# Plain float32 TensorE steps of a GLA stage put next to each other, and the end of the cross samples' chain moved into that stage

## The chip, the cores and the metric

The kernel runs on one core of one Trainium2 chip. The metric is the device time of one execution in microseconds (us). Three executions of the kernel before took 1443.68 us in the median (1443.25 to 1445.27). A fourth was taken with the hardware profiler: 1445.01 us, with a span of 1443.3 us from the first to the last instruction on the core.

## What is computed

One layer of a hybrid decoder, for 1024 prompt tokens and 8 sample tokens (one token each, with caches), width 1024. All branches read the same normalised input:

```python
h = rmsnorm(x, norm_gain)
q, k, v, gla_g, a_lr, u, pool_g, xq, xg, merge = split(h @ w_in)
z = a_lr @ w_a2 + b_a                       # the "logits" of the forget gate, rank 16
log_a = log_sigmoid(z) / 16
o, S = gla_chunked(q, k, v, log_a, S0)      # gated linear attention, 4 heads, 128 x 256
p, new_hist = multiscale_pool(u, hist, ...) # trailing means, a linear map for each of 4 groups
c = cross_attn(xq, mem_k, mem_v)            # 4 heads of 256, 256 memory tokens
merged = sum over the branches of sigmoid(merge) * (branch * silu(gate)) @ w_branch
y = rmsnorm(x + merged @ w_out, final_gain)
```

Outputs are both `y`, the prompt's memory keys and values, and the new GLA and pool states.

## The kernel before, in words

**The spine.** The input projection is 40 column blocks ("pairs") of `w_in`, each done as seven products of blocks (a scheme of Strassen's kind). `seq` lists 280 products, `run_product` (L547) does one. A product has two halves; a half (`product`, L537) is 12 matmuls of 128x258, four times the three of `mm3` (L240: hi*hi, hi*lo, lo*hi, lines 242 to 244). The operands of `mm3` are float32r: a value is split into a rounded half and a rest (`split`, L220: one ScalarE copy, one VectorE subtraction, lines 223 and 224), and three float32r products stand for one float32 product.

**What is woven in.** After each half product, `fill` (L1244) runs a little of a side stream. A stream is a Python generator that emits some instructions and yields a cost; `Stream.run` (L1229) takes steps until the sum of the costs reaches 493 * (half - 28) / 329, so about 1.5 of cost go with one half. All steps that fall to one half are emitted with no half between them. Stream 0 is `mix`: first `cross_steps` (cross-attention of the prompt, with the samples' chain `cross_sample` woven in), then `gla_steps` (GLA of the prompt, with `gla_sample` woven in). Stream 1, `pool_steps`, begins when stream 0 is over.

**What sets the order.** The order on TensorE and on the SyncE queue (SP: all loads) is the order in which the program emits. The orders of VectorE (DVE), ScalarE (ACT) and GpSimd (POOL) are picked at build time by a list scheduler. Every engine runs its list in order.

**The GLA stage before.** There are 16 chunks n of 256 tokens (4 heads x 4). For each n, `gla_steps` (L1069) does, with a yield behind each:
- `gla_gates(n+1)` (L904; 5): one plain float32 matmul of 128x256 (L907, the logits), then a long chain of 12 VectorE and 7 ScalarE steps that ends in L935, the scaled keys;
- `gla_split(n)` and `gla_within` of the first half of chunk n (L938; 2): two float32 matmuls on column tiles of 64 (L944, L945), a float32 transpose of the scaled keys (L946), a mask (L947), a split into `ak`;
- `gla_recur` of the second half of chunk n-1 (L952; 2): six float32r matmuls, and one plain float32 one (L963) with the state;
- `gla_within` of the second half of chunk n (2); the loads of n+2 and n+1 and `gla_recur` of the first half of chunk n (2); `gla_out(n-1)` (2).
Steps of the sample chain stand between them, one or two at a place.

**The cross stage's end.** Steps s = 0 to 17 emit scores(s), values(s-2) and weights(s-1), and five steps of `cross_sample` for each s. For s = 16 and 17 there are no scores left, and what is left of the last head's chain (softmax of the samples L791 to L798, its transpose L803, two groups of matmuls on column tiles of 32, L817, a last transpose L827) follows closely.

**Banks.** The side streams share two PSUM banks (`PZ`, tag pz) in turn; a bank comes free when ACT or DVE has read what the second last tile held. The spine has six (`PX`).

Of the kernel before, what the change touches and what calls it, by code (L numbers as in the profile page):

```python
# [18 lines left out]
P = 128  # L19
# [5 lines left out]
NH = 4  # L25
# [8 lines left out]
CT = 256  # L34
# [13 lines left out]
def trunk_kernel(ctx: ExitStack, tc: tile.TileContext,  # L48
# [3 lines left out]
    nc = tc.nc  # L52
# [46 lines left out]
    def PZ():  # L99
        return ps.tile([P, 512], F32, tag="pz", name="pz", bufs=2)  # L100
# [87 lines left out]
    w2 = cp.tile([P, 512], F32, name="w2")  # L188
# [488 lines left out]
    def perm8(ap):  # L677
        return ap.rearrange("p (i j) -> p i j", i=2)

    cross = {}  # L680

    def cross_load(h):
        cross["raw", h] = [loaded(mkv_scr[o][h], [2, DV], "mkv") for o in range(2)]
# [16 lines left out]
    def cross_scores(h, c):  # L700
        xh, xl = cross["q", h, c]
        mh, ml = cross["mk", h]
        t = PZ()
        for j in range(2):
            for i in range(2):
                cs = slice(j * P, (j + 1) * P)
                mm3(t[:, j * NM:(j + 1) * NM], xh[:, i, cs], xl[:, i, cs], mh[:, i], ml[:, i], i == 0, i == 1)
        nm = tiny(2, "nm")
        nc.vector.tensor_reduce(nm, t.rearrange("p (j m) -> p j m", j=2), axis=AX.X, op=ALU.max, negate=True)
        p = R([2, NM], name="p")  # L710
        sm = tiny(2, "sm")
        for j in range(2):
            act(p[:, j], t[:, j * NM:(j + 1) * NM], AF.Exp, bias=nm[:, j:j + 1], accum_out=sm[:, j:j + 1])
        nc.vector.reciprocal(sm, sm)
        for j in range(2):
            nc.vector.tensor_scalar(p[:, j], p[:, j], sm[:, j:j + 1], None, op0=ALU.mult)
        cross["p", h, c] = p
# [114 lines left out]
    def cross_steps():  # L832
        def scores(n):
            cross_scores(n // 4, n % 4)

        def memory(n):
            if n % 4 == 0:
                cross_memory(n // 4)

        def weights(n):  # L840
            cross_weights(n // 4, n % 4)

        def values(n):
            cross_values(n // 4, n % 4)

        samples = chain_of(cross_sample(h) for h in range(NH))
        cross_load(0)
        cross_memory(0)
        cross_fetch(0, 0)
        yield 2  # L850
        cross_queries(0, 0)
        cross_fetch(0, 1)
        for s in range(16 + 2):
            if s < 16:
                scores(s)
                yield 3
                if s + 1 < 16:
                    cross_queries(*divmod(s + 1, 4))
                if s + 2 < 16:
                    cross_fetch(*divmod(s + 2, 4))  # L860
            if s % 4 == 2 and s < 14:
                cross_load(s // 4 + 1)
            if s >= 1:
                yield next(samples, 0)
            if 0 <= s - 2:
                values(s - 2)
                yield 1.7
            if s >= 1:
                yield next(samples, 0)
            if s % 4 == 3 and s < 15:  # L870
                memory(s + 1)
                yield 2
            if 0 <= s - 1 < 16:
                weights(s - 1)
                yield 1.7
            for _ in range(3):
                if s >= 1:
                    yield next(samples, 0)
        yield from samples

    def chain_of(gens):
        for g in gens:
            yield from g


    gla = {}
# [9 lines left out]
    def gla_load(h, c):  # L896
        alc = wk.tile([P, CT], F32, tag="alc", name="alc", bufs=2)
        nc.sync.dma_start(out=alc, in_=al_scr[c // 2][:, (c % 2) * CT:(c % 2 + 1) * CT])
        kq = R([2, CT], name="kq")
        for j, scr in enumerate((k_scr, q_scr)):  # L900
            nc.sync.dma_start(out=kq[:, j], in_=scr[h // 2][:, 2 * (h % 2) + c // 2, (c % 2) * CT:(c % 2 + 1) * CT])
        gla["in", h, c] = alc, kq

    def gla_gates(h, c):  # L904
        alc, kq = gla["in", h, c]
        t = PZ()
        nc.tensor.matmul(t[:, :CT], lhsT=w2[:, h * P:(h + 1) * P], rhs=alc, start=True, stop=True)  # L907
        bz = R([2, CT], name="bz")
        b, z = bz[:, 0], bz[:, 1]
        gate_exps(t[:, :CT], CT, h, z, b)  # L910
        nc.vector.tensor_tensor_scan(b, smask, b, 0.0, op0=ALU.mult, op1=ALU.add)
        bl = b.rearrange("p (c e t) -> p c e t", e=2, t=64)[:, :, :, 63]
        dec = wk.tile([P, 4], F32, tag="dec", name="dec", bufs=3)
        d2 = dec.rearrange("p (c e) -> p c e", e=2)
        act(d2, bl, AF.Exp, scale=1.0 / TAU)
        decp = wk.tile([P, 2], F32, tag="decp", name="decp", bufs=3)
        nc.vector.tensor_tensor(decp, d2[:, :, 0], d2[:, :, 1], op=ALU.mult)
        blp = wk.tile([P, 4], F32, tag="blp", name="blp", bufs=2)
        blp2 = blp.rearrange("p (c e) -> p c e", e=2)
        nc.vector.tensor_copy(blp2[:, :, 1], bl[:, :, 1])  # L920
        nc.vector.tensor_tensor(blp2[:, :, 0], bl[:, :, 0], bl[:, :, 1], op=ALU.add)
        k, q = kq[:, 0], kq[:, 1]
        kiqi = R([2, CT], name="kiqi")
        ki, qi = kiqi[:, 0], kiqi[:, 1]
        act(z, b, AF.Exp, scale=1.0 / TAU, bias=lnq_c)
        nc.vector.tensor_tensor(q, q, z, op=ALU.mult)
        q4, qi4 = (x.rearrange("p (a e t) -> p a e t", e=2, t=64) for x in (q, qi))
        nc.vector.tensor_copy(qi4[:, :, 0], q4[:, :, 0])
        nc.vector.tensor_tensor(qi4[:, :, 1], q4[:, :, 1], d2[:, :, 0:1].to_broadcast([P, 2, 64]), op=ALU.mult)
        act(z, b, AF.Exp, scale=-1.0 / TAU)  # L930
        nc.vector.tensor_tensor(ki, k, z, op=ALU.mult)
        nc.vector.tensor_tensor(z.rearrange("p (c t) -> p c t", t=64), blp[:, :, None].to_broadcast([P, 4, 64]),
                                b.rearrange("p (c t) -> p c t", t=64), op=ALU.subtract)
        act(z, z, AF.Exp, scale=1.0 / TAU)
        nc.vector.tensor_tensor(k, k, z, op=ALU.mult)  # L935
        gla["g", h, c] = kq, kiqi, decp

    def gla_within(h, pr):  # L938

        c, cs = pr // 2, slice((pr % 2) * P, (pr % 2 + 1) * P)  # L940
        kq, kiqi, _ = gla["g", h, c]
        kt, qd, ki, qi = (x[:, cs] for x in (kq[:, 0], kq[:, 1], kiqi[:, 0], kiqi[:, 1]))
        t = PZ()
        nc.tensor.matmul(t[0:64, 0:P], lhsT=ki[:, 0:64], rhs=qi, start=True, stop=True)  # L944
        nc.tensor.matmul(t[64:P, 0:P], lhsT=ki[:, 64:P], rhs=qd, start=True, stop=True)  # L945
        nc.tensor.transpose(t[:, P:2 * P], kt, ident)  # L946
        nc.vector.copy_predicated(t[:, 0:P], nmask, zeros)  # L947
        ak = R([2, DV], F32R, name="ak")
        split(ak[:, 0], ak[:, 1], t[:, :DV])
        gla["w", h, pr] = ak[:, 0], ak[:, 1]  # L950
# [116 lines left out]
        yield 1.2  # L1067

    def gla_steps():  # L1069
        samples = chain_of(gla_sample(h) for h in range(NH))  # L1070
        N = 16
        gla_load(0, 0)
        gla_load(0, 1)
        gla_gates(0, 0)
        gla_values(0, 0)
        yield 5
        for n in range(N + 1):
            h, c = divmod(n, 4)
            ph, pc = divmod(n - 1, 4)
            if n + 1 < N:  # L1080
                gla_gates(*divmod(n + 1, 4))
                yield 5
            if n < N:
                gla_split(h, c)
                gla_within(h, 2 * c)
                yield 2
            if n > 0:
                gla_recur(ph, 2 * pc + 1)
                yield 2
                yield next(samples, 0)  # L1090
            if n < N:
                gla_within(h, 2 * c + 1)
                yield 2
                yield next(samples, 0)
                if n + 2 < N:
                    gla_load(*divmod(n + 2, 4))
                if n + 1 < N:
                    gla_values(*divmod(n + 1, 4))
                gla_recur(h, 2 * c)
                yield 2  # L1100
            if n > 0:
                gla_out(ph, pc)
                yield 2
            for _ in range(2):
                if n >= 1:
                    yield next(samples, 0)
        yield from samples


# [368 lines left out]
    for hf, order in enumerate(ORDERS):  # L1478
        for tb in order:
            m = P if tb < 8 else NS  # L1480
            if tb >= 8:
# [3 lines left out]
                for j in range(4):  # L1485
                    nc.tensor.matmul(ts[32 * j:32 * j + 32], lhsT=mgs[:, 4 * (tb - 8) + j], rhs=own.pop(0),
                                     start=tb == 8, stop=tb == 9)
# [15 lines left out]
            n, a = hf, 0  # L1503
            for b in ends:
                t = ts if tb == 8 else begun.pop(0) if begun else PX()
# [13 lines left out]
                n, a = n + 1, b  # L1519
# [46 lines left out]
```

## Time and profile before

| what | value |
|---|---|
| median of three executions | 1443.68 us |
| profiled execution, its span | 1445.01 us, 1443.3 us |
| TensorE busy (matmul records) | 1417.4 us, 98% of the span |
| VectorE, ScalarE, GpSimd busy | 916.2 us (63%), 679.0 us (47%), 222.1 us (15%) |
| logits L907, state matmul L963 | 32 and 56 records, first to last start 381.0 to 698.9 and 409.6 to 739.5 us |
| mean granted TensorE clock | 0.997 |

How to read the rows: the timeline gives the start, the duration, the engine, the line, the operation, out<-in and the shape; in brackets stands the idle time of that engine before the instruction and what ended it. A plain float32 matmul leaves two records (two passes), a float32r one leaves one. The ends of matmuls are modelled, so one matmul's place on the engine is read from start to start. In the window view, "PE busy" is followed by the other engines, the granted clock, and the DMA share.

### The profile page before, as it was taken

To read this page: it belongs to the slowest core of one execution; us is meant where nothing else is said; L and a number is where in the kernel's file an instruction comes from. 1 tells how busy PE (TensorE), PEld (TensorE's weight loads), DVE (VectorE), ACT (ScalarE), POOL (GpSimd) and SP (SyncE) were. 2 spreads that over 40 slices of the span, in tenths; PEclk is the share of its full clock that TensorE was granted. 3 is DMA by queue.
4 is the path that set the end of the run, shared out by engine and by line. 5 is a ranking of instruction groups with operands and counts; after the bars stand their busy time and mean duration, and the time that the engine had idled before them with its cause. 6 is when DMAs were issued, how large, how long until landed. Compare 5 with 4: busy or idle time off the path is not lost.

```text
span 1443.3 us, 28179 instructions
## 1 busy us (share of the span) xinstructions
PE 1417.4 (98%) x10689; PEld 1356.1 (94%) x10689; DVE 916.2 (63%) x2123; ACT 679.0 (47%) x1575; POOL 222.1 (15%) x401
## 2 busy tenths in 40 slices
PE   8999999999999999999999999999999999999998
PEld 6899999989899999999999999999999999999876
DVE  6954756666687777767766778785672434554436
ACT  6743544443465666656654445444472432233212
POOL 3211111124342121212221111111010000000000
PEclk9999999999999999999999999999999999999999
DMA  9355665656656363554654455454694777632633
GB/s 329 125 165 169 217 218 187 207 175 165 198 155 193 115 192 129 182 176 126 187 167 150 149 188 170 159 184 163 204 298 134 234 257 249 234 104 79 224 118 116
DMA packets 183507, 259.42 MB, mean 180 GB/s; under 512 B 22204, under 2 KB 132564, under 8 KB 183364
## 3 DMA queue, kind: packets, MB, share of 16 engines
q1 hardware_dynamic: 159900, 183.87, 41.5%
q0 software_dynamic: 23328, 73.56, 14.7%
q8 instruction: 84, 1.38, 0.4%
q14 instruction: 51, 0.42, 0.1%
q10 hardware_dynamic: 144, 0.20, 0.0%
HBM read 180.47 MB, written 77.56 MB: 179 GB/s over the span
## 4 chain that ended last, share of the span: by engine, by line
PE 88%; DMA 5%; DVE 5%; issue 1%; ACT 1%; SPq 0%; POOL 0%; DVEq 0%; ACTq 0%; POOLq 0%
PE px L242 25%; PE px L243 25%; PE px L244 25%; DMA qb<-xqs 3%; PE pz L244 2%; PE pz L243 2%; PE pz L242 2%; DMA raw<-in_w_in_dram 1%; DVE kc L777 1%; PE pz L963 1%; PE pz L404 1%; PE pz L944 1%; PE pz L817 1%; PE pz L946 1%; PE pz L907 0%
## 5 line engine op out<-in xcount | busy, mean ns | idle before, releaser
L244 PE MATMUL px<-bh,wbl 128*128 128x384 f32 (+1 forms) x576 | 184.1, 320 | 0.0
L243 PE MATMUL px<-bl,wbh 128*128 128x384 f32 (+1 forms) x576 | 184.1, 320 | 0.0
L242 PE MATMUL px<-bh,wbh 128*128 128x384 f32 (+1 forms) x576 | 183.7, 319 | 0.0
L554 ACT ACTIVATE r<-px 128x258 f32<-128x258 f32 x240 | 89.9, 375 | 47.4 <-PE px L244 46.9
L242 PEld LDWEIGHTS px<-bh,wbh 128*128 128x128 f32 x576 | 108.3, 188 | 0.0
L243 PEld LDWEIGHTS px<-bl,wbh 128*128 128x128 f32 x576 | 108.2, 188 | 0.0
L244 PEld LDWEIGHTS px<-bh,wbl 128*128 128x128 f32 x576 | 108.2, 188 | 0.0
L242 PE MATMUL px<-ot,s1h 128*128 128x258 f32 x320 | 94.1, 294 | 0.0
L242 PE MATMUL px<-o,a12h 128*128 128x258 f32 x320 | 93.4, 292 | 0.0
L242 PE MATMUL px<-ot,s3h 128*128 128x258 f32 x320 | 93.2, 291 | 0.0
L242 PE MATMUL px<-o,s4h 128*128 128x258 f32 x320 | 93.0, 291 | 0.2 <-DVE c L636 0.2
L242 PE MATMUL px<-o,a11h 128*128 128x258 f32 x320 | 92.8, 290 | 0.0
L242 PE MATMUL px<-ot,a22h 128*128 128x258 f32 x320 | 92.6, 289 | 0.0
L242 PE MATMUL px<-ot,s2h 128*128 128x258 f32 x320 | 92.2, 288 | 0.0
L243 PE MATMUL px<-o,a11h 128*128 128x258 f32 x320 | 91.1, 285 | 0.3 <-DVE o L224 0.3
L243 PE MATMUL px<-o,a12h 128*128 128x258 f32 x320 | 91.1, 285 | 0.0
L244 PE MATMUL px<-o,a12l 128*128 128x258 f32 x320 | 91.0, 284 | 0.0
L244 PE MATMUL px<-ot,s1l 128*128 128x258 f32 x320 | 90.9, 284 | 0.0
L243 PE MATMUL px<-ot,s1h 128*128 128x258 f32 x320 | 90.8, 284 | 0.0
L244 PE MATMUL px<-o,a11l 128*128 128x258 f32 x320 | 90.6, 283 | 0.0
L243 PE MATMUL px<-ot,s2h 128*128 128x258 f32 x320 | 90.1, 281 | 0.5 <-DVE ot L224 0.5
L243 PE MATMUL px<-ot,a22h 128*128 128x258 f32 x320 | 90.5, 283 | 0.0
(471 smaller groups left out, 4634.3 us busy)
## 6 DMA issues: line engine op xcount, KB each, us to landing
raw<-in_w_in_dram SPq DMA_DIRECT2D x80, 512.0 KB, 4.0
msc<-c POOLq DMA_DIRECT2D x24, 516.0 KB, 4.8
brsc<-c POOLq DMA_DIRECT2D x24, 516.0 KB, 3.7
sig<-msc SPq DMA_DIRECT2D x24, 516.0 KB, 6.0
brr<-brsc SPq DMA_DIRECT2D x48, 256.0 KB, 5.2
wbr<-in_w_branch_dram SPq DMA_DIRECT2D x24, 512.0 KB, 5.5
acc<-sig POOLq DMA_DIRECT2D x16, 516.0 KB, 5.2
acc<-acc SPq DMA_DIRECT2D x16, 516.0 KB, 7.0
```

What stands on the lines that cost most here:

```text
L242: nc.tensor.matmul(out, lhsT=lh, rhs=rh, start=start, stop=False, skip_group_check=more)
L243: nc.tensor.matmul(out, lhsT=lh, rhs=rl, start=False, stop=False, skip_group_check=more)
L244: nc.tensor.matmul(out, lhsT=ll, rhs=rh, start=False, stop=stop, skip_group_check=more)
L404: nc.tensor.matmul(t[:, :DV], lhsT=memT[k // 2][:, k % 2, a * P:(a + 1) * P], rhs=raw[k // 2][:, k % 2], start=k == 0, stop=k == NK - 1)
L554: nc.scalar.activation(r, acc[c][:, :QT], AF.Copy)
L777: nc.vector.tensor_tensor_reduce(kc[:, a, :], kc[:, a, :], qb[:, bb, :], scale=1.0, scalar=0.0, op0=ALU.mult, op1=ALU.add, accum_out=sc[:, ...
L817: nc.tensor.matmul(t[32 * j:32 * j + 32, :DV], lhsT=pm[:, a, 4 * i + j, :], rhs=vc[j][:, a, :], start=a == 0, stop=a == 1)
L944: nc.tensor.matmul(t[0:64, 0:P], lhsT=ki[:, 0:64], rhs=qi, start=True, stop=True)
L946: nc.tensor.transpose(t[:, P:2 * P], kt, ident)
L963: nc.tensor.matmul(to, lhsT=kiqi[:, 1, cs], rhs=st, start=False, stop=True)
```

## The change

Three edits. (1) `gla_gates` loses its matmul to a function of its own, `gla_logits`. (2) The loop of `gla_steps` has three steps for each n in place of six: logits(n+1), split and first within of n, gates(n+1); then recur of the second half of n-1 directly followed by the second within of n; then the loads, recur of the first half of n, and out of n-1. Costs and places of the sample steps are set anew. (3) For s = 16 and 17 the cross stage takes two sample steps in place of five, and what is left of the chain runs ahead of the GLA samples in `gla_steps`.

```diff
-    cross = {}
+    cross, later = {}, []
...
-            for _ in range(3):
+            for _ in range(3 if s < 16 else 0):
                 if s >= 1:
                     yield next(samples, 0)
-        yield from samples
+        later.append(samples)
...
+    def gla_logits(h, c):
+        alc, _ = gla["in", h, c]
+        t = gla["lg", h, c] = PZ()
+        nc.tensor.matmul(t[:, :CT], lhsT=w2[:, h * P:(h + 1) * P], rhs=alc, start=True, stop=True)
+
     def gla_gates(h, c):
-        alc, kq = gla["in", h, c]
-        t = PZ()
-        nc.tensor.matmul(t[:, :CT], lhsT=w2[:, h * P:(h + 1) * P], rhs=alc, start=True, stop=True)
+        _, kq = gla["in", h, c]
+        t = gla["lg", h, c]
...
-        samples = chain_of(gla_sample(h) for h in range(NH))
+        samples = chain_of(later + [gla_sample(h) for h in range(NH)])
         N = 16
         gla_load(0, 0)
         gla_load(0, 1)
+        gla_logits(0, 0)
         gla_gates(0, 0)
         gla_values(0, 0)
         yield 5
         for n in range(N + 1):
...
             if n + 1 < N:
-                gla_gates(*divmod(n + 1, 4))
-                yield 5
+                gla_logits(*divmod(n + 1, 4))
             if n < N:
                 gla_split(h, c)
                 gla_within(h, 2 * c)
-                yield 2
+            if n + 1 < N:
+                gla_gates(*divmod(n + 1, 4))
+            if n < N:
+                yield 6 if n + 1 < N else 3
             if n > 0:
                 gla_recur(ph, 2 * pc + 1)
-                yield 2
+            if n < N:
+                gla_within(h, 2 * c + 1)
+            yield 5 if 0 < n < N else 3
+            if n >= 1:
+                yield next(samples, 0)
+            if 0 < n < N:
                 yield next(samples, 0)
             if n < N:
-                gla_within(h, 2 * c + 1)
-                yield 2
-                yield next(samples, 0)
                 if n + 2 < N:
                     gla_load(*divmod(n + 2, 4))
                 if n + 1 < N:
                     gla_values(*divmod(n + 1, 4))
                 gla_recur(h, 2 * c)
-                yield 2
             if n > 0:
                 gla_out(ph, pc)
-                yield 2
-            for _ in range(2):
-                if n >= 1:
-                    yield next(samples, 0)
+            yield 4 if 0 < n < N else 2
+            for _ in range(3 if n < 5 else 2):
+                yield next(samples, 0)
         yield from samples
```

## The prediction

> **What bounds the kernel now.** I read the page first, then the busy time by stretches, then TensorE's waits, and last the timeline around single steps.
>
> ```profile
> span 1443.3 us, 28179 instructions
> 400.00:740.00 340.00, 340.00 (x2779) 324.55 (x2778) 253.67 (x663) 209.45 (x585) 79.55 (x133) 1.00 0.53 161
> ```
>
> The second line is the GLA stage: TensorE is busy for all of its 340 us, at full clock, while DVE works for 254 us. So a step in this stage counts by the time that it takes from the stream of matmuls, and a wait can only be added there. Waits exist ahead of it, where the cross stage runs out:
>
> ```profile
> PE pz L803 <- DVE ps L798: 2.4, 1, 2.4
> PE pz L243 <- DVE pTl L224: 1.5, 1, 1.5
> PE pz L724 <- ACT xo L736: 1.1, 1, 1.1
> PE pz L1001 <- DVE ak L224: 0.7, 1, 0.7
> ```
>
> These are all of TensorE's waits from 330 to 400 us (total, times, longest), 5.7 us together. Adding up the yields by hand, with 1.5 of cost for a half product, tells which of them the change can reach: up to half 144 both programs emit the same, and L243 (values of step 14) and L724 (weights of step 15) lie there. So 2.6 us stay, and L803 and L1001 are within reach. The wait of L803 costs more than itself:
>
> ```profile
> 356.00:360.00 4.00, 3.21 (x25) 2.90 (x25) 3.92 (x13) 0.69 (x2) 2.22 (x4) 1.00 0.12 18
> ...
> 364.00:368.00 4.00, 1.61 (x9) 1.62 (x10) 3.90 (x10) 2.08 (x6) 0.14 (x1) 0.86 1.01 345
> 368.00:372.00 4.00, 4.00 (x33) 2.90 (x32) 0.40 (x1) 0.38 (x1) 0.00 (x0) 0.72 0.05 14
> ```
>
> The column behind POOL is the granted clock. Behind the 2.4 us it is 0.86 and then 0.72, which loses 4 * 0.14 + 4 * 0.28 = 1.7 us; the shorter waits of 1.5 and 1.1 us left it at 1.00.
>
> **Grouping the plain float32 steps.** What does a change between float32r and plain float32 cost?
>
> ```profile
> 39.84 3.62 PE L404 MATMUL pz<-wm,memT 128*128 128x256 f32 x16
> 33.51 0.38 PE L404 MATMUL pz<-wm,memT 128*128 128x256 f32 x1
> 33.81 0.42 PE L520 MATMUL pz<-h,wa 128*32 128x258 f32 x4
> ```
>
> Sixteen plain records of 128x256 in a row take 3.62 us, the last one 0.38 of it, so (3.62 - 0.38) / 15 = 0.216 us each, and a plain matmul of two records 0.43 us, with no change of kind in it. Now one that stands alone between float32r matmuls:
>
> ```profile
> 380.85 0.29 PE L243 MATMUL px<-o,a11h 128*128 128x258 f32 x1
> 380.97 0.28 PE L244 MATMUL px<-o,a11l 128*128 128x258 f32 x1
> 381.10 0.59 PE L907 MATMUL pz<-alc,w 128*128 128x256 f32 x2
> 381.34 0.47 PE L242 MATMUL px<-o,s4h 128*128 128x258 f32 x1
> 381.64 0.28 PE L243 MATMUL px<-o,s4h 128*128 128x258 f32 x1
> ```
>
> The pitch of float32r is 380.97 - 380.85 = 0.12 us. From 380.97 to 381.64 are 0.67 us; less two pitches, the logits took 0.43 us: the same as in a row. And a place where two plain steps happen to stand together already:
>
> ```profile
> 491.46 0.28 PE L244 MATMUL px<-o,a12l 128*128 128x258 f32 x1
> 491.58 0.60 PE L1063 MATMUL pz<-ident,os 128*128 128x128 f32 x4
> 492.01 0.60 PE L907 MATMUL pz<-alc,w 128*128 128x256 f32 x2
> 492.26 0.47 PE L242 MATMUL px<-ot,s2h 128*128 128x258 f32 x1
> 492.57 0.28 PE L243 MATMUL px<-ot,s2h 128*128 128x258 f32 x1
> ```
>
> From 492.01 to 492.57, less one pitch, the logits take 0.44 us. Nothing was saved by company, so grouping L907 and L963 (the same shape) as such is worth zero. What does carry an overhead is the within step, which works on column tiles:
>
> ```profile
> 482.72 0.29 PE L244 MATMUL px<-o,s4l 128*128 128x258 f32 x1
> 482.94 0.32 PE L944 MATMUL pz<-kiqi 128*64 128x128 f32 x1
> ...
> 483.31 0.33 PE L946 MATMUL pz<-ident,kq 128*128 128x128 f32 x1
> 483.39 0.36 PE L242 MATMUL px<-o,s4h 128*128 128x258 f32 x1
> 483.59 0.28 PE L243 MATMUL px<-o,s4h 128*128 128x258 f32 x1
> ```
>
> It takes 483.59 - 482.72 - 0.24 = 0.63 us, and 482.94 - 482.72 - 0.12 = 0.10 us of it pass before its first matmul. The change puts L907 or L963 before it in place of a float32r matmul, 30 times. The nearest row is L520 above, a tiled step behind a plain one: 33.51 + 0.216 = 33.73, and it starts at 33.81, after 0.08 us. So 0.02 * 30 = 0.6 us may go; I take **-0.5 us**. The bounds are 0 and, if the whole entry went, -0.10 * 30 = -3.0 us.
>
> The Trainium skill, TensorEngine Tiling (Array Packing), Tiling Modes, Key Properties, says that a change of tiling mode (not just of the tile) drains TensorE. By that rule the entry stays whatever stands before it, and this term is 0. The rows agree with it, 0.10 beside 0.08 us.
>
> **The cross tail.** By the yields, values(15) moves ahead of L803 (halves 146 and 147; before 148 and 146), and both L817 and L827 go into the GLA stage (159, 168, 172).
>
> ```profile
> 366.19 0.69 DVE L224 TENSOR_TENSOR pTl<-pz,pTh 128x512 fp32r<-128x512 f32 x1
> 366.39 0.26 PE L803 MATMUL pz<-ident,ps 8*128 8x8 f32 x2 [2.39 <-DVE ps L798]
> ```
>
> What values(15) reads, `pTl`, is ready at 366.19 + 0.69 = 366.88, behind the samples' softmax on DVE. So the wait of L803 does not go: values(15) takes it over and ends it 366.88 - 366.39 = 0.5 us later, with the same slow clock behind it: **+0.5 us**. If the schedulers put `pTl` first, the wait and the clock's loss go: -2.4 - 1.7 = -4.1 us. L1001 moves from half 161 to 180 and loses its wait: **-0.7 us** (bound 0). L817 and L827 take the same time in either stage.
>
> **The first chunk.** The cost behind the first gates stays 5, but before, gates(1) with 5 more came between it and the first within: halves 152 and 159. Now they are 148 and 151. Three halves of 12 * 0.12 are 4.3 us; with two logits (0.86), the entry (0.10) and the way to the transpose L946 (483.31 - 482.94 = 0.37), TensorE asks for the scaled keys 5.7 us after the first logits start. When are they there?
>
> ```profile
> 389.47 0.40 DVE L935 TENSOR_TENSOR kq<-kq,bz 128x256 f32<-128x256 f32 x1
> 400.70 0.59 PE L907 MATMUL pz<-alc,w 128*128 128x256 f32 x2
> 407.61 0.42 DVE L935 TENSOR_TENSOR kq<-kq,bz 128x256 f32<-128x256 f32 x1
> ```
>
> For the chunk whose logits start at 381.10 after 8.8 us, with a second chunk's chain mixed in; for that of 400.70 after 7.3 us. So a new wait of 1.6 to 3.1 us on 946; nearer to the second row, since the second chain now comes behind: **+1.9 us**. All of TensorE's queue stands behind it, the spine too. The Trainium skill, TensorE: Matmul & The Clock Gate, Part 1, says that the clock falls to half after an idle window of about 3.4 us. By that a wait of 1.9 us costs no clock, and the sum stays; the rows above are stricter, since 2.4 us were enough, so the upper bound is 3.1 + 1.7 = 4.8 us.
>
> **Banks.** In one place (half 213) a sample transpose L1001, the logits and the within now share one half, and the within needs the bank that the transpose has just filled. The nearest price is L1001's own wait for a bank: 0 to 0.7 us, **+0.4**.
>
> **The stage's end.** The last sample group L1048 and its transpose L1063 had three halves between them and now have two (357 and 359).
>
> ```profile
> 742.93 0.64 PE L1048 MATMUL pz<-s,pm 128*32 128x256 f32 x8
> 743.50 0.39 PE L242 MATMUL px<-ot,s2h 128*128 128x258 f32 x1
> ...
> 747.95 0.84 PE L1063 MATMUL pz<-ident,os 128*128 128x128 f32 x4
> ```
>
> From start to start were 5.0 us, with a chain of ACT and DVE steps between. Now 743.50 - 742.93 + 2 * 1.44 = 3.5 us pass: a wait of 0 to 1.5 us, **+1.2** since little slack is left in a chain that long. The pool stream starts two halves later and catches up by its own pace: 0.
>
> **The sum**: -0.5 + 0.5 - 0.7 + 1.9 + 0.4 + 1.2 = +2.8 us. On the profiled execution, 1445.01 us, that is 1447.8; that execution is 1.3 us above the median, so the median to expect is 1443.7 + 2.8 = **1446.5 us**. What a measurement of this kernel can tell from no change is about 0.2%, 2.9 us, so this lies at the edge of it.
>
> **The rivals.**
>
> *Grouping pays and the tail clears (faster).* All 30 entries vanish (-3.0) and `pTl` comes early (-4.1 in place of +0.5): -3.0 - 4.1 - 0.7 + 1.9 + 0.4 + 1.2 = -4.3, 1439.4 us. For it: these are the only places with anything to win. Against it: 0.08 beside 0.10 us. Chance 0.22.
>
> *The denser burst makes banks late (slower).* Split, mask, `ak` and gates are now emitted together.
>
> ```profile
> 636.32 0.33 PE L946 MATMUL pz<-ident,kq 128*128 128x128 f32 x1
> 641.27 0.42 DVE L224 TENSOR_TENSOR ak<-pz,ak 128x256 fp32r<-128x256 f32 x1
> ```
>
> This is the slowest release of a within's bank, 5.4 us. The second within takes the bank again after four halves (5.8), six float32r matmuls (0.72) and L963 (0.43): 6.9 us. It decides once gates steps get ahead and a release grows by over 1.5 us, as the chain above varied by 8.8 - 7.3. Five of the 15 chunks late by 1 us: +5 on the sum, 1451.5 us. Against it: the earlier emission comes first in the program. Chance 0.13.
>
> *It does nothing* because the steps stand together already: 1443.7 us. The rows show L907 and L944 each between spine matmuls, so 0.05.
>
> **How the numbers follow.** The forecast has 0.60; its terms' bounds without the two rivals (first chunk 1.6 to 4.8, end 0 to 1.5, banks 0 to 0.7, L1001 0 to -0.7, values(15) from -2.4) give some 1443 to 1450, of which 0.34 lie within 0.2% and 0.26 above. Within 0.2%: 0.34 + 0.05 = 0.39. Slower: 0.26 + 0.13 = 0.39. Faster: 0.22. The range reaches to both rivals' times and leaves about half of each out: 1439.5 to 1451.
>
> **What would show it.** Right: logits still 0.43 us and within 0.62 us in company; a wait on L243 of values(15) of about 3 us with the clock down behind it; waits on L944 or L946 of the first chunk near 2 us, on L1063 near 1 us; none on L1001 at the start. Wrong: within steps near 0.53 us, or no wait from 360 to 400 us (faster); waits on L944 or L963 in many chunks (slower).

## The result, and the profile after

The changed kernel takes 1452.18 us in the median of 4 executions (1451.01 to 1452.79), the kernel before 1443.47 (1442.29 to 1445.27, 4 executions beside it): a ratio of 1.0054, 95% interval 1.0041 to 1.0067. It is slower by some 8 us, beyond the range that was given.

All of TensorE's waits in the changed kernel from 330 to 420 us (total, times, longest), where the cross stage ends and the GLA stage begins:

```profile
PE pz L242 <- ACT pTh L223: 2.0, 1, 2.0
PE pz L950 <- DVE kq L939: 1.2, 1, 1.2
PE pz L724 <- ACT xo L736: 1.1, 1, 1.1
PE pz L907 <- DMA alc<-als: 0.7, 1, 0.7
PE pz L243 <- DVE pTl L224: 0.6, 2, 0.3
PE pz L948 <- DVE kiqi L935: 0.5, 1, 0.5
```

In the changed kernel the lines behind L907 have moved by four (L944 to L946 are L948 to L950, L963 is L967, L1048 and L1063 are L1052 and L1067), and L1127, the first matmul of the pool stream, is L1135. The waits of L803 and L1001 are gone. Values(15) waits for its weights `pTh` and `pTl` instead, 2.03 + 0.34 = 2.4 us (the other 0.3 us on `pTl` belongs to values(14)), and the first chunk's within for `kiqi` and `kq`, 1.7 us. The logits of the third chunk now wait 0.7 us for their load `alc`. Together these six are 6.1 us, against 5.7 before: the tail is no better, but it does not hold 8 us either. The next wait of any size stands where none was before, at the seam between the GLA stage and the pool stream. This is the only one from 735 to 775 us:

```profile
PE pz L1135 <- DMA hist<-in_state_pool_dram: 4.3, 1, 4.3
```

The window view of the same stretch (the column behind the engines is the granted clock), first of the kernel before, then of the changed one:

```profile
740.00:760.00 20.00, 20.00 (x170) 19.16 (x169) 13.07 (x42) 10.16 (x28) 4.92 (x10) 1.00 0.60 189
```

```profile
740.00:760.00 20.00, 15.65 (x117) 14.75 (x116) 8.98 (x28) 8.70 (x24) 4.52 (x10) 0.85 0.53 167
```

TensorE had no gap here before; now 4.35 of the 20 us are idle, and behind them the clock is down:

```profile
752.00:756.00 4.00, 0.67 (x4) 0.70 (x5) 0.43 (x1) 0.63 (x1) 0.00 (x0) 0.75 1.03 344
756.00:760.00 4.00, 4.00 (x21) 3.92 (x22) 1.46 (x6) 1.21 (x3) 0.54 (x1) 0.50 0.33 103
760.00:764.00 4.00, 4.00 (x32) 4.00 (x32) 2.31 (x9) 0.70 (x3) 0.74 (x1) 0.90 0.35 133
```

4 * 0.25 + 4 * 0.50 + 4 * 0.10 = 3.4 us are lost to it at most (part of the first window was idle anyway). The wait and the clock make up to 7.8 us, the size of the whole loss.

A second way to read the same: number the spine's half products from the first, and compare when the Nth starts in each kernel. Unlike a window, this does not mix stages that have slid against each other. The start in the profiled execution of before, and how much later (+) or earlier (-) it is in the others, in us, worked out from the starts of TensorE's rows, with the first half of each kernel laid on that of before:

| half | before | after | pool's loads early | before, pool late | carry only | logits apart |
|---|---|---|---|---|---|---|
| 144 | 357.56 | -5.39 | -1.34 | -2.10 | -4.00 | -2.43 |
| 155 | 384.38 | -3.34 | -2.10 | -2.91 | -5.77 | -3.33 |
| 160 | 392.53 | -1.86 | -0.62 | -2.91 | -0.37 | -1.86 |
| 200 | 465.46 | -1.15 | -0.44 | -2.91 | +0.68 | -1.73 |
| 358 | 748.55 | -1.03 | -1.02 | -3.18 | +4.54 | +0.07 |
| 362 | 755.79 | +6.52 | -0.53 | +4.54 | +4.53 | +0.56 |
| 500 | 982.53 | +6.52 | -0.53 | +4.50 | +4.53 | +0.56 |

(The last four columns are kernels of the experiments.) Up to half 144 the instructions are the same as before, so the -5.4 there is what one execution differs from another, not the change. From half 144 to 200, over the cross tail and the first chunk, the changed kernel falls back by 4.2 us in this pair of profiles. With the pool's loads early, where the steps up to half 200 are the same, the same stretch costs 0.9 us: what was lost there besides the waits is clock, and it differs between executions (the last section shows why). From half 200 to 358, most of the GLA stage with its grouped steps, the changed kernel moves by 0.1 us against before. Then 7.5 us appear within four halves, and they stay to the end.

Why did `hist` come late? The timeline of SP, the queue on which all loads are issued, in the kernel before and then in the changed one:

```profile
727.34 11.17 SPq L296 DMA_DIRECT2D raw<-in_w_in_dram  x2
738.61 0.45 SPq L670 DMA_DIRECT2D pwr<-in_pool_w_dram  x1
739.15 0.42 SPq L1116 DMA_DIRECT2D hist<-in_state_pool_dram  x1
...
751.66 0.37 SPq L296 DMA_DIRECT2D raw<-in_w_in_dram  x1
```

```profile
737.70 13.03 SPq L296 DMA_DIRECT2D raw<-in_w_in_dram  x2
750.78 0.50 SPq L670 DMA_DIRECT2D pwr<-in_pool_w_dram  x1
751.38 0.43 SPq L1124 DMA_DIRECT2D hist<-in_state_pool_dram  x1
```

The row `raw<-in_w_in_dram x2` is two loads of the spine's weights. The second cannot go out until DVE has done with an older buffer (what ended the wait was `ws`, L305, before, and `a22l`, L224, in the changed kernel), and SP, which runs its list in order, waits with it: 10.4 of the 11.17 us before, 12.2 of the 13.03 in the changed kernel. Before, the pool's first loads stood ahead of the load that waits until 751.66. In the changed kernel the yields of stream 0 add up to 495.8 instead of 492.8. The pace reaches that sum at half 359 instead of 357, so the first step of the pool stream falls to half 359 and not 358. Between these two halves the program prepares the next product, and emits its weight load. The pool's loads now stand behind it: `hist` is issued at 751.38 instead of 739.15, 12.2 us later, while its matmul moved by one half.

### The profile page after: what moved, and what is told of

Read it like the earlier page. It is cut to its first block, busy times and chain, and to the rows that moved or that the text cites. A ratio compares the mean times of both kernels' runs of the same rounds, so it can differ in the third digit from the quotient of the medians.

```text
span 1449.3 us, 28194 instructions
## 1 busy us (share of the span) xinstructions
PE 1419.4 (98%) x10689; PEld 1354.0 (93%) x10689; DVE 917.2 (63%) x2123; ACT 678.3 (47%) x1575; POOL 221.4 (15%) x401
## 4 chain that ended last, share of the span: by engine, by line
PE 85%; DMA 6%; DVE 5%; ACT 2%; issue 1%; SPq 1%; DVEq 0%; POOL 0%; ACTq 0%
PE px L242 25%; PE px L243 24%; PE px L244 24%; PE pz L243 2%; PE pz L244 2%; DMA qb<-xqs 2%; PE pz L242 2%; DMA raw<-in_w_in_dram 1%; DVE kc L777 1%; PE pz L967 1%; PE pz L948 1%; DMA x<-in_x_prompt_dram 1%; PE pz L950 1%; PE pz L817 0%; DVE ws L305 0%
## 5 line engine op out<-in xcount | busy, mean ns | idle before, releaser
L242 PE MATMUL px<-ot,s3h 128*128 128x258 f32 x320 | 92.5, 289 | 0.0
L242 PE MATMUL px<-o,a12h 128*128 128x258 f32 x320 | 92.1, 288 | 0.0
L244 PE MATMUL px<-ot,s3l 128*128 128x258 f32 x320 | 90.9, 284 | 0.0
L243 PE MATMUL px<-ot,s3h 128*128 128x258 f32 x320 | 90.8, 284 | 0.0
```

Of the source, the lines that this page charges most:

```text
L242: nc.tensor.matmul(out, lhsT=lh, rhs=rh, start=start, stop=False, skip_group_check=more)
L243: nc.tensor.matmul(out, lhsT=lh, rhs=rl, start=False, stop=False, skip_group_check=more)
L244: nc.tensor.matmul(out, lhsT=ll, rhs=rh, start=False, stop=stop, skip_group_check=more)
```

## The experiments

The theory: the loss is the pool stream's place on the SP queue; grouping is worth nothing, and the cross tail and the first chunk are nearly a draw. The rivals: the seam costs time wherever the loads stand; the carried chain is the cost; the denser emission of gates and logits is. Each experiment has a time of before from the same chip: 1443.38, 1443.02, 1442.45 and 1443.31 us in the four groups below.

**Is it the queue?** First, the changed kernel with nothing moved but the pool's two first loads, which are emitted with the GLA stage's last output, at half 355 in place of 359, and so ahead of the weight load between halves 358 and 359:

```diff
+            if n == N:
+                next(pool)
...
         fetched = group_fetch(0)
+        yield 0
         for g, w in enumerate(WINDOWS):
...
+    pool = pool_steps()
```

> The changed kernel, with the first two loads of the pool stream (pool_w and the pool history of group 0) issued with the last gla_out, so ahead of the next load of w_in on SyncE's queue; every TensorE step stays at its half. Theory (the queue position costs the time): the wait of 4.3 us on hist and the slow clock behind it go, about -7 us, 1445 us, and the waits at the first chunk stay. Rival (the denser GLA steps cost the time, the late loads only show it): within 2 us of the changed kernel, 1450 to 1453 us.

Measured: 1444.59 us, ratio 1.0009 (0.9996 to 1.0022). SP's timeline shows the order turned round:

```profile
738.27 0.46 SPq L670 DMA_DIRECT2D pwr<-in_pool_w_dram  x1
738.82 0.43 SPq L1126 DMA_DIRECT2D hist<-in_state_pool_dram  x1
750.47 0.38 SPq L296 DMA_DIRECT2D raw<-in_w_in_dram  x1
```

There is no wait of TensorE's from 735 to 775 us, and no jump in the table. What is left of the change is no difference that can be measured.

The converse, the kernel before with nothing but the pool's start moved to half 359:

```diff
-        if streams[0].over:
+        if streams[0].over and s >= 359:
```

> The kernel before, with the pool stream held back from half 358 to half 359, and nothing else changed. Theory: its first loads fall behind the load of w_in, hist comes late, and the time rises by 6 to 8 us to about 1450 us. Rival (denser GLA steps): one half later changes nothing, 1443 to 1445 us.

Measured: 1450.34 us, 1.0042 (1.0027 to 1.0057), with the same wait and SP row as in the changed kernel:

```profile
PE pz L1127 <- DMA hist<-in_state_pool_dram: 4.9, 1, 4.9
```

```profile
735.09 13.49 SPq L296 DMA_DIRECT2D raw<-in_w_in_dram  x2
```

So the loss can be taken out of the changed kernel and put into the old one with one emission that changes sides of a weight load. The queue is shown, and the rival that the seam costs as such has fallen.

**Does company save float32 time?** The same kernel as the first, with the logits moved away from the first within of each chunk again, 15 of the 30 groups (the loads early, the carry kept, the sum of the costs the same):

```diff
                 gla_logits(*divmod(n + 1, 4))
+                yield 2
...
-                yield 6 if n + 1 < N else 3
+                yield 4 if n + 1 < N else 3
```

> The changed kernel with the pool's first loads early, and with the logits taken apart from the within steps again (2 of cost between them, 4 in place of 6 behind; 15 of the 30 groups undone). Theory (company saves nothing on TensorE): the logits take 0.43 us and the within 0.63 us, as together 1.06 us, and the time is that of the first experiment within 2 us, 1443 to 1447 us. Rival (a group saves the entry of the column tiles, 0.10 us each): the two sum to 1.16 us, 1.5 us slower than the first experiment.

Measured: 1444.75 us, 1.0014 (1.0004 to 1.0025), against 1.0009 grouped. The timeline of the changed kernel at one such place, logits and within together:

```profile
417.16 0.28 PE L244 MATMUL px<-ot,s2l 128*128 128x258 f32 x1
417.28 0.59 PE L907 MATMUL pz<-alc,w 128*128 128x256 f32 x2
417.80 0.32 PE L948 MATMUL pz<-kiqi 128*64 128x128 f32 x1
...
418.17 0.33 PE L950 MATMUL pz<-ident,kq 128*128 128x128 f32 x1
418.26 0.37 PE L242 MATMUL px<-ot,s2h 128*128 128x258 f32 x1
418.46 0.28 PE L243 MATMUL px<-ot,s2h 128*128 128x258 f32 x1
```

and with the logits apart, first they, then the within:

```profile
415.98 0.28 PE L244 MATMUL px<-ot,s2l 128*128 128x258 f32 x1
416.10 0.59 PE L907 MATMUL pz<-alc,w 128*128 128x256 f32 x2
416.35 0.47 PE L242 MATMUL px<-ot,s2h 128*128 128x258 f32 x1
416.65 0.28 PE L243 MATMUL px<-ot,s2h 128*128 128x258 f32 x1
...
417.84 0.28 PE L244 MATMUL px<-ot,s2l 128*128 128x258 f32 x1
418.05 0.32 PE L948 MATMUL pz<-kiqi 128*64 128x128 f32 x1
...
418.50 0.37 PE L242 MATMUL px<-ot,s1h 128*128 128x258 f32 x1
418.71 0.28 PE L243 MATMUL px<-ot,s1h 128*128 128x258 f32 x1
```

Together: 418.46 - 417.16 less two pitches of 0.12 is 1.06 us. Apart: 416.65 - 415.98 - 0.24 = 0.43, and 418.71 - 417.84 - 0.24 = 0.63, again 1.06. The within's entry stays, behind a plain matmul too: 417.80 - 417.28 - 0.43 = 0.09 us. The other places agree: in the kernel before the entry behind float32r is 0.09 us at all 32 places (0.085 to 0.097); in the changed kernel it is 0.09 us behind the logits (median of 13 places) and 0.09 to 0.10 us behind the state matmul L967 (14 places), which is the other half of the groups.

**The carry alone.** The kernel before, with only the rest of the samples' chain carried into the GLA stage:

```diff
-            for _ in range(3):
+            for _ in range(3 if s < 16 else 0):
                 if s >= 1:
                     yield next(samples, 0)
-        yield from samples
+        later.append(samples)
...
-        samples = chain_of(gla_sample(h) for h in range(NH))
+        samples = chain_of(later + [gla_sample(h) for h in range(NH)])
```

> The kernel before with only the end of the cross samples' chain carried into the GLA stage; the GLA steps keep their old grouping and costs, and the pool stream starts at half 358. Theory: values of step 15 take over the wait of L803 (2 to 2.6 us, with the clock behind it), the wait of L1001 goes, and there is no wait at the first within since 7 halves lie between: 1442 to 1444 us. Rival (carrying the chain clears the tail): the waits from 360 to 400 us go, 1439 to 1441 us.

Measured: 1453.36 us, 1.0064 (1.0042 to 1.0086): a miss by 10 us. The table shows +5.4 us between halves 155 and 160, and the profile gives the reason: a wait of TensorE's and SP's row ahead of the load that it waits for.

```profile
PE pz L907 <- DMA alc<-als: 3.6, 1, 3.6
```

```profile
370.28 16.04 SPq L296 DMA_DIRECT2D raw<-in_w_in_dram  x2
386.41 0.49 SPq L898 DMA_DIRECT2D alc<-als  x1
```

The profiled execution is one of the fastest of the six (1449.24; they spread from 1448.99 to 1457.28), so it holds 4 to 6 of the 10 us; the rest is in no trace. With fewer steps left in the cross stage the GLA stage starts four halves earlier (148 in place of 152), and now the input of its third chunk falls behind a weight load that waits. It is the same mechanism at another seam. Issuing this one load earlier is the test:

```diff
         gla_gates(0, 0)
+        gla_load(0, 2)
...
-                if n + 2 < N:
+                if 0 < n and n + 2 < N:
                     gla_load(
```

> The experiment that carries the chain alone, with the load of chunk 2 issued together with those of chunks 0 and 1, ahead of two loads of w_in on SyncE's queue. Theory (there too a load stood behind a w_in load that waits for its buffer): the wait of 3.6 us on alc and the slow clock behind it go, 4 to 6 us below that experiment, 1447 to 1449 us. Rival (the carried chain's own steps cost the time): within 2 us of it, 1451 to 1455 us.

Measured: 1450.61 us, 1.0047 (1.0032 to 1.0062). The wait for `alc` is gone, and from half 155 to 160 this kernel loses 1.25 us instead of 5.4. Yet the median falls by only 2.8 us, and since the two intervals overlap even that is not clear. Other waits stay: 3.9 us of the within L944 for a bank that `ak` holds, 1.3 us of L1063 for `os`. So the carry alone has a price beyond this one load. It puts more sample steps into a GLA stage that draws no more of them per chunk, while the changed kernel draws three for the first chunks; that the samples run late for this reason fits the waits, but was not tried by itself.

**The rest without the carry.** The changed kernel with the pool's loads early and the chain left in the cross stage:

```diff
-            for _ in range(3 if s < 16 else 0):
+            for _ in range(3):
...
-        later.append(samples)
+        yield from samples
```

> The changed GLA grouping alone: the cross stage runs its chain to the end as in the kernel before, and the pool's first loads are issued ahead of the w_in load, so that their queue position doesn't count. Theory: grouping saves nothing on TensorE (logits 0.43 and within 0.63 us stay additive), the first chunk waits about 2 us and slows the clock: 1445 to 1448 us. Rival (grouping saves the entries of the column-tile steps): 3 us below the kernel before, 1440 to 1441 us.

Measured: 1452.43 us, 1.006 (1.0041 to 1.0078), a miss as well. The first chunk loses 3.2 us between halves 155 and 160 (waits of 1.4 for `kiqi` and 1.0 for `kq`). Waits of 1.0 for `ak` (half 169) and 1.5 for `alc` (half 232) come later, and a wait of 3.2 us for `dfh` appears in the pool stream, behind which the clock goes down (+6.7 us between halves 365 and 370). Why DVE and ACT come to `dfh` late there was not settled. The two halves of the change cannot be priced one by one and added: each alone loses more than both together with the pool's loads early.

**Can a wait be bought off with spacing?** Three kernels change the pace. The first is the changed one with the loads early, three more of cost behind weights(15), five more behind the first gates, and a little less in each chunk:

```diff
-                yield 1.7
+                yield 1.7 if s < 16 else 4.7
...
-        yield 5
+        yield 10
...
-            yield 4 if 0 < n < N else 2
+            yield 3.5 if 0 < n < N else 2
```

> The changed kernel with the pool's first loads issued early as in the first experiment, and two waits spaced out: 3 more of cost (two halves) between weights and values of step 15, and 10 in place of 5 behind the first gates; the last cost of each chunk is 3.5 in place of 4, so that the stage ends where it did. Theory (the waits at values of step 15 and at the first within are all that the change still costs): about 3 us on values and 1.7 us on the within go, 1439 to 1442 us, faster than the kernel before. Rival (other waits take their place, since the chains on VectorE and ScalarE are late by themselves): no gain on the first experiment, 1443 to 1446 us.

Measured: 1452.75 us, 1.0068 (1.005 to 1.0086). Values(15) waits no longer (the 0.9 us left on `pTl` is values(14)), and 5.4 us were won on before between halves 144 and 148. They were lost at once: the first chunk's `alc` fell behind a weight load that waited for 9 us.

```profile
355.38 9.96 SPq L296 DMA_DIRECT2D raw<-in_w_in_dram  x2
365.39 2.81 SPq L670 DMA_DIRECT2D vc<-in_cache_mem_v_dram  x4
368.24 0.95 SPq L898 DMA_DIRECT2D alc<-als  x1
```

TensorE waited 6.0 us for it. The second is the kernel before with the same space behind weights(15), and the total work set to 496 to match:

```diff
-                yield 1.7
+                yield 1.7 if s < 16 else 4.7
...
-    WORK_A, WORK_B = 493.0
+    WORK_A, WORK_B = 496.0
```

> The kernel before with 3 more of cost behind the last weights of the cross stage, and a total of 496 in place of 493, so that the pool stream starts where it did. Theory (the tail waits because its steps follow too closely): the wait of L803, 2.4 us, and the slow clock behind it, 1.7 us, go: 1439 to 1441 us. Rival (the wait moves to the next step of the chain): 1443 to 1445 us.

The third is the changed kernel with the total work at 496 and nothing else:

> The changed kernel with one number changed: the work of stream 0 is set to 496 in place of 493, which is its sum, so that the stream ends at half 357 and the pool stream starts ahead of the w_in load again. Theory (queue position): the wait on hist goes without any load being moved, 1443 to 1446 us. Rival (what helped in the first experiment was the early issue of the loads, not their place behind the w_in load): 1449 to 1453 us.

Measured: 1449.04 us, 1.004 (1.0027 to 1.0053), and 1455.88 us, 1.009 (1.0075 to 1.0106). Neither time answers what the kernel was made for. The total sets the pace of stream 0 from half 28 on, so every step of the cross stage moves: by half 100 both are already behind, by 6.5 and 4.7 us, long before the place in question. What they do show: in the second the wait of L803 is gone, and 5.1 us are won between halves 146 and 148; by half 152, 3.7 of them are lost again, with waits of L817 for `pm` and `vc`, and later waits of 2.1 us for `alc` and 1.6 for `c` stand in L907's way; in the third there is no wait for `hist` and no jump from half 358 to 362 (+11.56 and +11.59), as the theory says, and the time still went up.

**A version that fills the tail.** If TensorE idles at the end of the cross stage because nothing else is ready, the first chunk can be made ready there. The changed kernel, pool's loads early, with the first chunk's loads and values issued at step 15 of the cross stage, and its logits and gates behind weights(15):

```diff
+            if s == 15:
+                gla_load(0, 0)
+                gla_load(0, 1)
+                gla_values(0, 0)
...
                 weights(s - 1)
                 yield 1.7
+                if s == 16:
+                    gla_logits(0, 0)
+                    gla_gates(0, 0)
+                    yield 3
...
-        gla_load(0, 0)
-        gla_load(0, 1)
-        gla_logits(0, 0)
-        gla_gates(0, 0)
-        gla_values(0, 0)
-        yield 5
+        yield 2
```

> The changed kernel with the pool's first loads early, and with the GLA stage's first loads issued at step 15 of the cross stage and its first logits and gates put between weights and values of step 15 (with 3 of cost behind them, and 2 in place of 5 at the stage's start, so that all later steps keep their halves). Theory (the waits at values of step 15, about 3 us, and at the first within, 1.7 us, are what the change still costs, provided that no load falls behind a w_in load): 1439 to 1442 us. Rival (the chains on VectorE and ScalarE are late by themselves, or another wait appears): 1443 to 1446 us.

Measured: 1435.89 us, 0.9953 (0.9938 to 0.9968), faster than both kernels and than expected. Is that the change's doing? Two more kernels have the same early first chunk and early pool loads: one on the kernel before, with neither part of the change, and one on the carry alone.

> The kernel before with the first chunk's loads, values and gates issued while the cross stage still runs (as in the version that took 1435.9), and the pool's first loads issued with the last output of the GLA stage. Neither part of the change is in it. Theory (the gain of that version comes from filling TensorE's waits at the end of the cross stage, and the change has no part in it): 1435 to 1438. Rival (carrying the samples' chain makes the room: with the chain left in the cross stage, the wait of L803, 2.4 us, and the slow clock behind it, 1.7 us, stay): 1439 to 1442.

> The same with the rest of the samples' chain carried into the GLA stage as well, so that only the grouping of the float32 steps is left out of the version that took 1435.9. Theory (grouping is worth nothing): 1435 to 1437. Rival (the order that came with the grouping gives the samples' and gates' chains the time they need: without it a wait for a bank or a late decay load, 2 to 4 us, appears as in the version with the carry alone): 1438 to 1441.

Measured: 1436.03 us, 0.9946 (0.9932 to 0.9961), for the first, and 1448.45 us, 1.0032 (1.0019 to 1.0045), for the second. With neither part of the change the gain is the same, so the change has no part in it, and the rival of the carry that makes room falls. The window view of the first of the two shows the tail without a gap, at full clock; it is the same in the other two kernels:

```profile
340.00:360.00 20.00, 20.00 (x169) 19.91 (x168) 15.77 (x42) 9.54 (x22) 12.32 (x20) 1.00 0.85 258
360.00:380.00 20.00, 20.00 (x174) 17.97 (x174) 12.83 (x32) 9.60 (x24) 6.36 (x11) 1.00 0.53 143
```

Where do the 7 us come from? By the starts of the halves, all three kernels with the first chunk early win 5.0 us on before between halves 146 and 148, and the two kernels with space behind weights(15) won 5.1 and 5.4 there. So this part is the space: the 3 of cost put two halves of the spine there, while the first logits are 0.43 us of TensorE's work. What the early loads add is that the gain is kept; they are emitted at half 134 (in the first spaced kernel at 150), and the first chunk's `alc` is not late. Another 3.1 us are won between halves 143 and 146, ahead of every TensorE step that was moved. There the waits of values(14) and weights(15) (1.5 and 1.1 us before) are gone, because DVE runs its list in another order: before, `pTl` stood behind a `kc` step that waited 4.1 us for `qb`. Why the order came out that way was not tried.

The second was worse than either expectation, although by half 152 it is 8.1 us ahead of before. Its largest wait is at the stage's end:

```profile
PE pz L1055 <- DVE s L1038: 6.6, 1, 6.6
```

There DVE sat idle for 6.0 us for the samples' values `vb`, which SP issued at 742.28 us. In this kernel alone the pool's early loads (half 349) stand ahead of the samples' last loads (half 352), and both draw on the same four buffers (L119 of the kernel before). With the carry alone, where the pool's loads come last, there is no such wait. So the early pool loads are the likely cause, though it was not tried, and this run does not tell whether the order that came with the grouping is worth anything.

## Why the prediction was wrong, point by point

The failed step is this one: "The pool stream starts two halves later and catches up by its own pace: 0." It was priced at nothing without a row behind it, and it was worth more than the other terms together. The later start itself is indeed free: with the loads early the stream's first matmul stays at half 359, and nothing is lost there. What it missed is that the pool stream's first emission is a load, and that the program emits a weight load between the two halves. In the trace this cost 7.5 us (half 358 to 362); undone, it takes the ratio from 1.0054 to 1.0009; done to the kernel before, it makes 1.0042. The price could be read before: `727.34 11.17 SPq L296` says that SP stands still for over 10 us at such a load, with `hist` right behind it.

The other terms, without this one, gave +2.8 us; the kernel with the loads early shows 0.0009 * 1443.4 = +1.3 us (-0.6 to +3.2), so this sum was neither confirmed nor refuted as a whole. (The bounds of its terms add up to 1441.7 and 1450.7 us, not to "some 1443 to 1450".)
- *Drains, -0.5*: 0. The entry of 0.10 us was 0.09 behind a plain matmul, and 1.06 us of work is 1.06 together or apart. This agrees with the Trainium skill, TensorEngine Tiling (Array Packing), Tiling Modes, Key Properties: a change of tiling mode drains TensorE. The rival that had these drains vanish falls with it.
- *Values(15), +0.5*: right that the wait is taken over, but the 0.5 us more did not come: L803's 2.4 us became 2.4 on `pTh` and `pTl`. The clock behind them costs 3.41 * 0.50 = 1.7 us, the figure that was carried over.
- *L1001, -0.7*: right, it is gone. The 0.7 us of the third chunk's logits for `alc` were not foreseen.
- *First chunk, +1.9*: 1.7 us were measured, 0.5 on `kiqi` and 1.2 on `kq`. The working holds too: TensorE asked 374.90 - 367.40 - 1.7 = 5.8 us after the first logits (5.7 foretold), and the keys were there after 7.5 (7.3 foretold). What the sum left out is the clock, 1.7 us more in the changed kernel's profile. By the rule that the prediction set beside this term so short a wait costs no clock; here it did. The windows, cut where the granted clock changes, show it, the first two rows at values(15), the last two at the first chunk:

```profile
358.03:361.44 3.41, 1.04 (x7) 0.64 (x6) 3.25 (x8) 2.07 (x6) 0.55 (x1) 1.00 1.05 343
361.44:364.85 3.41, 3.41 (x18) 3.41 (x18) 1.17 (x2) 0.62 (x2) 0.21 (x1) 0.50 1.05 369
...
371.68:375.09 3.41, 1.74 (x14) 1.10 (x13) 3.38 (x10) 2.07 (x6) 1.90 (x4) 1.00 0.22 50
375.09:378.51 3.42, 3.42 (x18) 3.42 (x18) 2.02 (x5) 1.41 (x5) 3.41 (x6) 0.50 0.65 96
```

- *The bank at half 213, +0.4*: nothing at that place. A wait of that kind (L948 on ACT's read of `vs`, L1007), 0.5 us, stands at half 316 instead, and not in the kernel with the loads early.
- *The stage's end, +1.2*: nothing. In the changed kernel L1067 starts at 750.33, 0.12 us behind the matmul ahead of it at 750.21. The chain of 5.0 us held slack after all. In other kernels (carry alone, with and without the early load; the changed one spaced, or with total work 496) the wait is there, 1.2 to 2.2 us on `os`.
- *The denser burst* fell: from 400 to 740 us the changed kernel has 0.7 us of waits, in two places.

## What to carry to other kernels

When an edit changes costs or yields, list the loads whose place on an in-order queue it changes, and look in the trace for the loads on that queue that wait for a buffer: a load that slips behind one of them comes later by that whole wait, here 9 to 16 us, however small the edit. Compare two traces by the starts of the same numbered step rather than by windows; that gave the place at once. Two more halves between a step and the one that waits for it won 5 us at this seam in five kernels, but the two that only spaced lost it to what came behind; it was kept where the next stage's loads had been issued early as well (-7 us, with and without the change).

## What the runs showed of the hardware

The same small waits do not cost the same clock each time. With the loads early, values(15) and the first chunk wait as in the changed kernel (2.2 us on `pTh`, 1.2 on `kq`), but the granted clock stays at 1.00 there, where the changed kernel has 0.50 twice for 3.41 us. The traces tell why. The clock goes down in whole stretches of 3.41 us (1.7 us lost), 6.83 or, once, 10.24 us, and all of them lie on one grid in steps of 3.41 us, which starts elsewhere in each execution. Cut along its grid, the kernel with the loads early reads:

```profile
360.30:363.72 3.42, 2.25 (x19) 2.04 (x18) 1.40 (x4) 0.01 (x1) 2.40 (x4) 1.00 0.98 318
363.72:367.13 3.41, 2.00 (x14) 1.80 (x15) 3.07 (x6) 2.07 (x6) 0.00 (x0) 1.00 1.06 362
367.13:370.54 3.41, 3.41 (x29) 3.23 (x28) 0.18 (x1) 0.75 (x2) 0.68 (x1) 1.00 0.94 323
```

The border at 363.72 cuts its wait in two, 1.2 and 1.4 us of idle time; in the changed kernel 2.4 and 1.7 us fell into one stretch each. Over the 14 traces, from some 10 us in to 1425 us, a stretch at full clock with 1.8 us or more of idle time was always followed by one at 0.50 and one with 1.6 us or less never, while in between both occur. So the loss behind a wait of about 2 us was 0 or 1.7 us, by where it fell. Behind the 4.35 us the clock was at 0.50 for two stretches, 3.4 us lost. The Trainium skill, TensorE: Matmul & The Clock Gate, Part 1, calls the window that is watched free-running, so that its phase differs between executions; these rows agree. It has the clock fall after an idle window of about 3.4 us; here about half of one was enough.
